# A chunk inverse with compacted blocks and wide transposes, and three smaller edits around it, in a fused hybrid decoder trunk

## Chip, cores and metric

One Trainium2 chip, one core. The metric is the device time of one launch in microseconds; lower is better. The kernel before takes 1242.85 us (median of 3 runs, 1240.87 to 1247.7).

## What is computed

Two residual layers on 512 tokens of width 1024, in float32. Only layer 0 matters here. Its input projection is split between an RWKV-7 time mix (8 heads of 64) and a stick-breaking attention (8 heads of 64); both outputs are concatenated and projected. A mixture of experts follows, then layer 1 (a gated linear recurrence) and a second mixture of experts.

```python
def rwkv7_time_mix(p, w0, decay_up, a0, iclr_up, gate_up, ...):
    ...
    w_log = -jax.nn.softplus(-(w0 + jnp.tanh(xw) @ decay_up)) - 0.5
    decay = jnp.exp(-jnp.exp(w_log))
    a = jax.nn.sigmoid(a0 + xa @ iclr_up)
    ...
    def step(S, inp):
        r_t, w_t, k_t, v_t, a_t, b_t = inp
        sa = jnp.einsum('bhvk,bhk->bhv', S, a_t)
        S = S * w_t[:, :, None, :] + sa[..., None] * b_t[:, :, None, :] + v_t[..., None] * k_t[:, :, None, :]
        return S, jnp.einsum('bhvk,bhk->bhv', S, r_t)
```

The kernel computes the recurrence in chunks of 64 tokens. Within a chunk the terms `sa` depend on one another through a strictly triangular 64x64 matrix, so each of the 64 chunk-and-head pairs (8 heads, 8 chunks) needs the inverse of a unit triangular 64x64 matrix.

## The kernel before, in words

Layouts. Two heads lie together on the 128 partitions (s = 0 on 0 to 63, s = 1 on 64 to 127). `AMa` holds the triangular matrices of all 4 head pairs and 8 chunks, 32 chunk slots of 2x64 columns. `ps` banks of PSUM are 128x512 float32, with tags: `pj` (2 banks, projections), `rw` (3 banks), `at` (2), `o` (1).

Order of layer 0. `norm_even` normalizes; `lora` (L368 to L395) makes the decay and rate gates; `pair` for 4 head pairs projects r, k, v and scales them, and its `chunks` (L478 to L498) makes the triangular matrices; `qkv` for 4 head pairs (L691 to L719) projects q, k and v of the attention; `inverse` (L500 to L553) inverts; `values` (L555 to L592) multiplies with v; then `step` and `attend` run together in an order that is written out by hand.

What sets the order. Outside that hand-written part a planner at build time interleaves what is independent, using estimates of each instruction's time; the source order is not the order of the queues. Each engine then works through its own queue strictly in that order. In the profile, `inverse` runs beside the projections of `qkv`, because the last head pair's matrices are ready early in `qkv`.

A projection is 24 matmuls (L325, L326, L327: 8 blocks of the contraction, each as high-high, high-low and low-high, since float32 is split into two parts). Its weights are cast by ScalarE (L297) and the remainder made by VectorE (L298). For q and k, `qkv` squares the result (L704), averages it over the head by a matmul (L706), takes Ln (L707) and Exp (L708) on ScalarE, and multiplies on VectorE (L709), which is what empties the `pj` bank. For v it copies (L715), transposes on TensorE (L718) and copies out of PSUM (L719, VectorE).

`inverse` has three parts:

- Diagonal blocks. The four 32x32 diagonal blocks of a pair's two matrices lie on the four 32-partition groups. Four 32-partition transposes (L511) bring them to `z`, one element of a block per partition. `XT` is set to the identity (L512, L513, GpSimd). Then 31 steps of a forward substitution, each a product with a broadcast row (L519) and a reduction (L521) over up to 31x31 elements, run on VectorE.
- Back. Six transposes (L528, four; L530, two) return the blocks to `AMa` and to `TT`.
- Off-diagonal blocks. 32x32 matmuls (L540), copies by ScalarE (L542), 32x32 matmuls (L549), copies by VectorE (L551).

`values` transposes v (L571, L575) into `UV`, then multiplies: one 128x128 product per pair and chunk (L585) computes both heads at once, of which the two diagonal 64x64 blocks are kept (L587 on ScalarE, L588 on VectorE); L591 clears the other halves of `AMa`.

`lora` keeps the two weight matrices (64 rows each) in one buffer padded by zeros to 128 rows, so that each product is a 128-row matmul (L388, L391), followed by a sigmoid (L389, L392).

Of the kernel before, what the change touches and what calls it, by code (L numbers as in the profile page):

```python
# [18 lines left out]
T = 512  # L19
# [140 lines left out]
class Kern:  # L160
# [207 lines left out]
    def lora(self):  # L368
        nc, ar, I = self.nc, self.ar, self.I
        self.L1, self.G1, self.G2 = ar.get(T), ar.get(T), ar.get(T)  # L370

        du = ar.get(2 * T)
        dv = du.f(2, T)
        nc.gpsimd.memset(dv[64:128, 0], 0.0)
        nc.gpsimd.memset(dv[0:64, 1], 0.0)
        nc.sync.dma_start(dv[0:64, 0], I["decay_up"][0])
        nc.sync.dma_start(dv[64:128, 1], I["iclr_up"][0])
        sig = []
        self.shifted(LORA, self.L1.f())
        sig.append(nc.scalar.activation(self.L1.f()[0:64], self.L1.f()[0:64], AF.Tanh))  # L380
        self.shifted(1664, self.G1.f())
        sig.append(nc.scalar.activation(self.G1.f(), self.G1.f(), AF.Sigmoid))
        self.shifted(1696, self.G2.f())
        sig.append(nc.scalar.activation(self.G2.f(), self.G2.f(), AF.Sigmoid))
        self.SG, self.AA = ar.get(4 * T), ar.get(4 * T)
        for p in range(4):
            z = self.bank("rw")
            nc.tensor.matmul(z, dv[:, 0, p * 128:p * 128 + 128], self.L1.f(), start=True, stop=True)  # L388
            sig.append(nc.scalar.activation(self.SG.f(4, T)[:, p], z, AF.Sigmoid, bias=self.v("w0", p)))  # L389
            z = self.bank("rw")  # L390
            nc.tensor.matmul(z, dv[:, 1, p * 128:p * 128 + 128], self.L1.f(), start=True, stop=True)  # L391
            sig.append(nc.scalar.activation(self.AA.f(4, T)[:, p], z, AF.Sigmoid, bias=self.v("a0", p)))  # L392
        du.free()
        self.L1.free()
        self.switch(sig)  # L395
# [104 lines left out]
    def inverse(self):  # L500
# [1 line left out]
        nc, ar = self.nc, self.ar  # L502
        X = [self.AMa.f(32, 2, 64)[:, :, s] for s in range(2)]

        Z, XT = ar.get(1024), ar.get(1024)
        z, xt = Z.f(32, 32), XT.f(32, 32)
        for G in range(4):
            q = slice(32 * G, 32 * G + 32)
            s, g = divmod(G, 2)
            src = X[s][q, :, 32 * g:32 * g + 32].rearrange("p c i -> p i c")  # L510
            nc.vector.transpose(z[q], src)  # L511
        nc.gpsimd.memset(XT.f(), 0.0)  # L512
        nc.gpsimd.memset(XT.f()[:, 0:1024:33], 1.0)  # L513
        tmp = ar.get(1024)
        for i in range(1, 32):

            w = i
            tv = tmp.f()[:, 0:i * w].rearrange("p (r j) -> p r j", r=w)
            nc.vector.tensor_tensor(tv, xt[:, 0:i, 0:w].rearrange("p j r -> p r j"),  # L519
                                    z[:, i:i + 1, 0:i].to_broadcast([128, w, i]), OP.mult)  # L520
            nc.vector.tensor_reduce(xt[:, i, 0:w], tv, AX.X, OP.add)  # L521
        tmp.free()
        Z.free()
        TT = ar.get(1024)
        for G in range(4):
            q = slice(32 * G, 32 * G + 32)
            s, g = divmod(G, 2)
            nc.vector.transpose(X[s][q, :, 32 * g:32 * g + 32].rearrange("p c i -> p i c"), xt[q])  # L528
            if g == 0:
                nc.vector.transpose(TT.f(32, 32)[q].rearrange("p c r -> p r c"), xt[q].rearrange("p i r -> p r i"))  # L530
        XT.free()

        W = ar.get(1024)
# [9 lines left out]
        for half in range(2):  # L543
            for s in range(2):
                b = self.bank("rw")
                lo, hi = slice(s * 64, s * 64 + 32), slice(s * 64 + 32, s * 64 + 64)
                for i in range(16):
                    c = half * 16 + i
                    nc.tensor.matmul(b[lo, i * 32:i * 32 + 32], W.f(32, 32)[hi, c], X[s][hi, c, 32:64],  # L549
                                     start=True, stop=True, tile_position=(s * 64 + 32, s * 64))  # L550
                nc.vector.tensor_copy(X[s][lo, half * 16:half * 16 + 16, 32:64], b[lo].rearrange("p (c i) -> p c i", c=16))  # L551
        W.free()
        TT.free()  # L553

    def values(self):  # L555
# [23 lines left out]
        RV, AM = self.RV.f(4, 8, 64), self.AMa.f(4, 8, 2, 64)  # L579
        for p in range(4):  # L580
            for g in range(2):
                b = self.bank("rw").rearrange("p (c s v) -> p c s v", c=4, s=2)
                for i in range(4):
                    c = g * 4 + i
                    nc.tensor.matmul(b[:, i].rearrange("p s v -> p (s v)"), AM[:, p, c].rearrange("p s i -> p (s i)"),  # L585
                                     UV[:, c, p].rearrange("p s v -> p (s v)"), start=True, stop=True)
                nc.scalar.activation(RV[0:64, p, g * 4:g * 4 + 4], b[0:64, :, 0], AF.Copy)  # L587
                nc.vector.tensor_copy(RV[64:128, p, g * 4:g * 4 + 4], b[64:128, :, 1])  # L588

            for s, e in enumerate((nc.gpsimd, nc.vector)):  # L590
                e.memset(AM[64 - s * 64:128 - s * 64, p, :, s], 0.0)  # L591
# [103 lines left out]
    def qkv(self, p):  # L695
# [20 lines left out]
        m = self.bank("at")  # L716
        for t in range(4):
            nc.tensor.transpose(m[:, t * 128:t * 128 + 128], v[:, t * 128:t * 128 + 128], self.ident)  # L718
        nc.vector.tensor_copy(self.VT[p].f(4, 128), m.rearrange("p (t x) -> p t x", t=4))  # L719

    def beside(self, p):

# [963 lines left out]
```

## Time and profile before

| | |
|---|---|
| median of 3 runs | 1242.85 us (1240.87 to 1247.7) |
| the profiled execution's own time | 1241.28 us |
| its span, first to last instruction | 1239.6 us |
| TensorE busy | 1166.2 us, 94% |
| VectorE busy | 1013.6 us, 82% |
| ScalarE busy | 795.6 us, 64% |
| GpSimd busy | 486.8 us, 39% |
| mean granted TensorE clock | 0.982 of full |

Durations are those of one profiled execution. A matmul's own duration includes its pipeline; the distance of two starts is what it costs in a row. PE is TensorE, PEld its weight loads, DVE VectorE, ACT ScalarE, POOL GpSimd, SP the engine that issues most DMAs. A float32 matmul shows as two passes.

### The profile page before, as it was taken

The page shows a single profiled execution, that of the slowest core. Times are in us where ns is not written, and L with a number is a line of the kernel's source. Part 1 is how long each engine was busy: PE and PEld are TensorE (multiplying, and loading weights), DVE is VectorE, ACT ScalarE, POOL GpSimd, SP SyncE. Part 2 cuts the span into 40 slices and gives each one's busy share as a digit, 9 for nine tenths or more (in the row PEclk, how much of TensorE's full clock was granted, in tenths as well). Part 3 has the DMA queues.
Part 4 walks back from the last instruction along what each step waited for, and adds up shares of the span by engine and source line. Part 5 has one row for each costly group of instructions (what it writes and reads, how often), then busy time and mean ns, then how long its engine had stood idle before and what let it go on. Part 6 is the DMA issues. An engine that isn't in the chain of part 4 may idle for free. (4 is left out here: it accounts for less than half of the span.)

```text
span 1239.6 us, 18201 instructions
## 1 busy us (share of the span) xinstructions
PE 1166.2 (94%) x6718; PEld 861.0 (69%) x6719; DVE 1013.6 (82%) x1292; ACT 795.6 (64%) x1063; POOL 486.8 (39%) x321
## 2 busy tenths in 40 slices
PE   6999998999998799999999899999988999999997
PEld 5777766877676577777776676677766777777764
DVE  5387899687767699999998565698667999999986
ACT  6533333388544688888888464566446888888883
POOL 8043200211011366677765211210113557767753
PEclk9999999899998899999999999999998999999999
DMA  6312221014965899999995612267478999999964
GB/s 170 85 51 68 68 68 35 2 26 138 342 238 209 282 343 364 355 357 354 355 347 186 187 51 68 69 203 269 162 250 311 342 365 366 345 346 352 345 232 147
DMA packets 152390, 274.45 MB, mean 221 GB/s; under 512 B 8172, under 2 KB 59053, under 8 KB 152295
## 3 DMA queue, kind: packets, MB, share of 16 engines
q1 hardware_dynamic: 142438, 247.85, 57.8%
q0 software_dynamic: 7840, 18.04, 6.2%
q10 hardware_dynamic: 2016, 7.34, 1.5%
q8 instruction: 54, 0.88, 0.3%
q14 instruction: 42, 0.34, 0.1%
HBM read 258.80 MB, written 22.28 MB: 227 GB/s over the span
## 5 line engine op out<-in xcount | busy, mean ns | idle before, releaser
L297 ACT ACTIVATE R<-A 128x1024 fp32r<-128x1024 f32 (+1 forms) x451 | 473.2, 1053 | 206.0 <-PE ps_pj L1362 67.2
L298 DVE TENSOR_TENSOR R<-A,R 128x1024 fp32r<-128x1024 f32 (+1 forms) x362 | 494.0, 1398 | 76.8 <-ACT R L297 72.9
L298 POOL TENSOR_TENSOR R<-A,R 128x1024 fp32r<-128x1024 f32 x89 | 257.3, 2890 | 245.5 <-ACT R L297 241.2
L1363 PE MATMUL ps_pj<-R 128*96 128x512 f32 x512 | 205.3, 401 | 9.9 <-DVE R L298 9.9
L1361 PE MATMUL ps_pj<-R 128*96 128x512 f32 x512 | 205.9, 402 | 0.0
L1362 PE MATMUL ps_pj<-R 128*96 128x512 f32 x512 | 204.0, 398 | 0.0
L325 PE MATMUL ps_pj<-R 128*128 128x512 f32 x296 | 121.7, 411 | 10.0 <-DVE A L709 9.3
L327 PE MATMUL ps_pj<-R 128*128 128x512 f32 x296 | 119.5, 404 | 3.5 <-DVE R L298 3.5
L326 PE MATMUL ps_pj<-R 128*128 128x512 f32 x296 | 121.1, 409 | 0.0
L1363 PEld LDWEIGHTS ps_pj<-R 128*96 128x96 f32 x512 | 84.1, 164 | 47.0 <-DVE R L298 10.8
L1362 PEld LDWEIGHTS ps_pj<-R 128*96 128x96 f32 x512 | 84.2, 164 | 35.4 <-DVE R L298 0.4
L1388 PE MATMUL ps_at<-R 128*96 128x512 f32 x256 | 103.7, 407 | 4.9 <-PEq L1583 1.8
L1361 PEld LDWEIGHTS ps_pj<-R 128*96 128x96 f32 x512 | 84.3, 165 | 33.9
L1389 PE MATMUL ps_at<-R 128*96 128x512 f32 x256 | 101.6, 397 | 0.0
L1390 PE MATMUL ps_at<-R 128*96 128x512 f32 x256 | 101.5, 397 | 0.0
L325 PEld LDWEIGHTS ps_pj<-R 128*128 128x128 f32 x296 | 56.5, 191 | 27.7 <-DVE A L709 11.3
L327 PEld LDWEIGHTS ps_pj<-R 128*128 128x128 f32 x296 | 56.4, 190 | 20.5 <-DVE R L298 5.7
L1397 POOL DMA_INDIRECT YD<-A x30 | 67.3, 2243 | 4.8 <-issue 2.2
L326 PEld LDWEIGHTS ps_pj<-R 128*128 128x128 f32 x296 | 56.5, 191 | 14.8 <-issue 4.1
L1164 POOL TENSOR_TENSOR A<-A 128x1024 f32<-128x1024 f32 x6 | 16.2, 2716 | 126.9 <-DVE A L870 87.3
L1266 DVE TENSOR_TENSOR A<-A 128x384 bf16<-128x384 f32 x32 | 60.0, 1886 | 0.0
L298 DVE TENSOR_TENSOR R<-ps_rw,R 128x384 fp32r<-128x384 f32 x92 | 47.7, 543 | 14.6 <-ACT R L297 14.5
(445 smaller groups left out, 2010.6 us busy)
## 6 DMA issues: line engine op xcount, KB each, us to landing
A<-in_exp_w_up_dram SPq DMA_DIRECT2D x61, 1024.0 KB
A<-in_exp_w_down_dram SPq DMA_DIRECT2D x61, 1024.0 KB
A<-in_exp_w_gate_dram SPq DMA_DIRECT2D x59, 1024.0 KB
A<-in_w_in_even_dram SPq DMA_DIRECT2D x27, 512.0 KB
A<-in_w_in_odd_dram SPq DMA_DIRECT2D x20, 512.0 KB
S<-in_exp_w_gate_dram SPq DMA_DIRECT2D x5, 1024.0 KB
A<-in_w_out_odd_dram SPq DMA_DIRECT2D x10, 512.0 KB
A<-in_x_dram SPq DMA_DIRECT2D x8, 512.0 KB
```

The source lines that it names most:

```text
L297: a = self.nc.scalar.activation(hi, src, AF.Copy)
L298: return a, (eng or self.nc.vector).tensor_tensor(lo, src, hi.bitcast(F32), OP.subtract)
L325: nc.tensor.matmul(p[0:n], hi[:, k], Hh[:, k], start=k == 0, stop=False)
L326: nc.tensor.matmul(p[0:n], hi[:, k], Hl[:, k], start=False, stop=False)
L327: nc.tensor.matmul(p[0:n], lo[:, k], Hh[:, k], start=False, stop=k == KD - 1)
L1361: self.nc.tensor.matmul(b, xh[:, k], hi, start=k == 0, stop=False)
L1362: self.nc.tensor.matmul(b, xl[:, k], hi, start=False, stop=False)
L1363: self.nc.tensor.matmul(b, xh[:, k], lo, start=False, stop=k == KD - 1)
L1388: nc.tensor.matmul(yb[n], hh[:, k], hi[:, cs], start=k == 0, stop=False)
L1389: nc.tensor.matmul(yb[n], hl[:, k], hi[:, cs], start=False, stop=False)
L1390: nc.tensor.matmul(yb[n], hh[:, k], lo[:, cs], start=False, stop=k == 3)
L1397: self.nc.gpsimd.indirect_dma_start(out=self.YD[l][:, :], out_offset=bass.IndirectOffsetOnAxis(ap=ix[0:SL], axis=0), in_=y.rearrange("p a ...
```

## The change

Four edits, all in layer 0:

- `lora`: the padded buffer is replaced by one of half the size, the two memsets go, and the two products of a step use 64 rows each, on the lower and the upper half of the array, into two banks taken together.
- `inverse`: ScalarE first copies the four diagonal blocks into one contiguous buffer (`tmp`), and one 128-partition transpose makes `z`. The result is kept by columns: the product now reads `xt` in sequence and the reduction writes a column with a step of 32 elements. One 128-partition transpose brings the result back into `tmp`, four ScalarE copies put the blocks into `AMa`, and one 128-partition transpose makes `TT`. Of the four copies out of PSUM at the end, two go to ScalarE.
- `values`: each 128x128 product becomes two of 128 rows by 64 columns, one per head, into the lower and upper half of the bank's partitions.
- `qkv`: the copy of v out of PSUM is done by ScalarE.

```diff
@@ lora
-        du = ar.get(2 * T)
-        dv = du.f(2, T)
-        nc.gpsimd.memset(dv[64:128, 0], 0.0)
-        nc.gpsimd.memset(dv[0:64, 1], 0.0)
-        nc.sync.dma_start(dv[0:64, 0], I["decay_up"][0])
-        nc.sync.dma_start(dv[64:128, 1], I["iclr_up"][0])
+        du = ar.get(T)
+        dv, q = du.f(), [slice(s * 64, s * 64 + 64) for s in range(2)]
+        for s, name in enumerate(("decay_up", "iclr_up")):
+            nc.sync.dma_start(dv[q[s]], I[name][0])
...
-            z = self.bank("rw")
-            nc.tensor.matmul(z, dv[:, 0, p * 128:p * 128 + 128], self.L1.f(), start=True, stop=True)
-            sig.append(nc.scalar.activation(self.SG.f(4, T)[:, p], z, AF.Sigmoid, bias=self.v("w0", p)))
-            z = self.bank("rw")
-            nc.tensor.matmul(z, dv[:, 1, p * 128:p * 128 + 128], self.L1.f(), start=True, stop=True)
-            sig.append(nc.scalar.activation(self.AA.f(4, T)[:, p], z, AF.Sigmoid, bias=self.v("a0", p)))
+            z = [self.bank("rw") for _ in q]
+            for s in range(2):
+                nc.tensor.matmul(z[s], dv[q[s], p * 128:p * 128 + 128], self.L1.f()[q[s]], start=True, stop=True)
+            for b, dst, name in zip(z, (self.SG, self.AA), ("w0", "a0")):
+                sig.append(nc.scalar.activation(dst.f(4, T)[:, p], b, AF.Sigmoid, bias=self.v(name, p)))
@@ inverse
-        for G in range(4):
-            q = slice(32 * G, 32 * G + 32)
-            s, g = divmod(G, 2)
-            src = X[s][q, :, 32 * g:32 * g + 32].rearrange("p c i -> p i c")
-            nc.vector.transpose(z[q], src)
+        diag = [(slice(32 * G, 32 * G + 32), G // 2, slice(32 * (G % 2), 32 * (G % 2) + 32)) for G in range(4)]
+        for q, s, g in diag:
+            nc.scalar.activation(tmp.f(32, 32)[q], X[s][q, :, g], AF.Copy)
+        nc.vector.transpose(z, tmp.f(32, 32).rearrange("p c i -> p i c"))
...
-            w = i
-            tv = tmp.f()[:, 0:i * w].rearrange("p (r j) -> p r j", r=w)
-            nc.vector.tensor_tensor(tv, xt[:, 0:i, 0:w].rearrange("p j r -> p r j"),
-                                    z[:, i:i + 1, 0:i].to_broadcast([128, w, i]), OP.mult)
-            nc.vector.tensor_reduce(xt[:, i, 0:w], tv, AX.X, OP.add)
-        tmp.free()
+            tv = tmp.f()[:, 0:i * i].rearrange("p (r j) -> p r j", r=i)
+            nc.vector.tensor_tensor(tv, xt[:, 0:i, 0:i], z[:, i:i + 1, 0:i].to_broadcast([128, i, i]), OP.mult)
+            nc.vector.tensor_reduce(xt[:, 0:i, i], tv, AX.X, OP.add)
+        nc.vector.transpose(tmp.f(32, 32).rearrange("p c i -> p i c"), xt.rearrange("p r i -> p i r"))
+        for q, s, g in diag:
+            nc.scalar.activation(X[s][q, :, g], tmp.f(32, 32)[q], AF.Copy)
         Z.free()
         TT = ar.get(1024)
-        for G in range(4):
-            q = slice(32 * G, 32 * G + 32)
-            s, g = divmod(G, 2)
-            nc.vector.transpose(X[s][q, :, 32 * g:32 * g + 32].rearrange("p c i -> p i c"), xt[q])
-            if g == 0:
-                nc.vector.transpose(TT.f(32, 32)[q].rearrange("p c r -> p r c"), xt[q].rearrange("p i r -> p r i"))
+        nc.vector.transpose(TT.f(32, 32).rearrange("p c r -> p r c"), xt)
+        tmp.free()
...
-                nc.vector.tensor_copy(X[s][lo, half * 16:half * 16 + 16, 32:64], b[lo].rearrange("p (c i) -> p c i", c=16))
+                (nc.vector.tensor_copy if s else nc.scalar.copy)(X[s][lo, half * 16:half * 16 + 16, 32:64], b[lo].rearrange("p (c i) -> p c i", c=16))
@@ values
-                b = self.bank("rw").rearrange("p (c s v) -> p c s v", c=4, s=2)
+                b = self.bank("rw")[:, 0:256].rearrange("p (c v) -> p c v", c=4)
                 for i in range(4):
                     c = g * 4 + i
-                    nc.tensor.matmul(b[:, i].rearrange("p s v -> p (s v)"), AM[:, p, c].rearrange("p s i -> p (s i)"),
-                                     UV[:, c, p].rearrange("p s v -> p (s v)"), start=True, stop=True)
-                nc.scalar.activation(RV[0:64, p, g * 4:g * 4 + 4], b[0:64, :, 0], AF.Copy)
-                nc.vector.tensor_copy(RV[64:128, p, g * 4:g * 4 + 4], b[64:128, :, 1])
+                    for s in range(2):
+                        nc.tensor.matmul(b[s * 64:s * 64 + 64, i], AM[:, p, c, s], UV[:, c, p, s], start=True, stop=True)
+                nc.scalar.activation(RV[0:64, p, g * 4:g * 4 + 4], b[0:64], AF.Copy)
+                nc.vector.tensor_copy(RV[64:128, p, g * 4:g * 4 + 4], b[64:128])
@@ qkv
-        nc.vector.tensor_copy(self.VT[p].f(4, 128), m.rearrange("p (t x) -> p t x", t=4))
+        nc.scalar.activation(self.VT[p].f(4, 128), m.rearrange("p (t x) -> p t x", t=4), AF.Copy)
```

## Rows read from the trace of the kernel before

**Rows 1.** The page, part 1: busy us of each engine.
```profile
PE 1166.2 (94%) x6718; PEld 861.0 (69%) x6719; DVE 1013.6 (82%) x1292; ACT 795.6 (64%) x1063; POOL 486.8 (39%) x321
```

**Rows 2.** Waits of TensorE, 0 to 300 us: total us, times, longest.
```profile
PE ps_pj L325 <- DVE A L709: 9.3, 3, 3.9
```

**Rows 3.** Windows: length, busy PE, PEld, DVE, ACT, POOL, clock, DMA share, GB/s.
```profile
149.20:226.30 77.10, 67.81 (x268) 50.99 (x266) 73.61 (x90) 22.88 (x33) 2.35 (x1) 0.93 0.16 43
226.30:235.70 9.40, 9.40 (x266) 8.98 (x265) 2.74 (x4) 3.79 (x6) 3.99 (x4) 0.97 0.01 3
```

**Rows 4.** Timeline, ScalarE and VectorE near the first stop: start, us.
```profile
164.15 0.63 ACT L708 ACTIVATE A<-A 128x512 f32<-128x512 f32 x1
...
169.48 0.74 DVE L709 SCALAR_TENSOR_TENSOR A<-ps_pj,A 128x512 f32<-128x512 f32 x1
```

**Rows 5.** Timeline, TensorE at the three stops: start, us, [idle before].
```profile
170.28 0.80 PE L325 MATMUL ps_pj<-R 128*128 128x512 f32 x1 [3.00 <-DVE A L709]
...
193.39 0.50 PE L325 MATMUL ps_pj<-R 128*128 128x512 f32 x1 [2.40 <-DVE A L709]
...
218.17 0.80 PE L325 MATMUL ps_pj<-R 128*128 128x512 f32 x1 [3.87 <-DVE A L709]
```

**Rows 6.** VectorE by line and shape: busy us, mean ns; 149 to 226, L551 later.
```profile
L511 DVE STREAM_TRANSPOSE A<-A 32x1024 f32<-32x1024 f32 x4 | 8.1, 2016 | 0.0
L528 DVE STREAM_TRANSPOSE A<-A 32x1024 f32<-32x1024 f32 x4 | 8.0, 1989 | 0.1
L530 DVE STREAM_TRANSPOSE A<-A 32x1024 f32<-32x1024 f32 x2 | 3.9, 1958 | 0.0
L519 DVE TENSOR_TENSOR A<-A 128x961 f32<-128x961 f32 x1 | 2.0, 1991 | 0.0
L719 DVE COPY S<-ps_at 128x512 f32<-128x512 f32 x2 | 1.4, 690 | 0.0
L521 DVE TENSOR_REDUCE A<-A 128x31 f32<-128x961 f32 x1 | 1.2, 1153 | 0.0
...
L551 DVE COPY A<-ps_rw 32x512 f32<-32x512 f32 x4 | 2.7, 684 | 2.2 <-PE ps_rw L549 2.2
```

**Rows 7.** Windows of L519 alone (first) and of L521 alone (second).
```profile
149.80:225.30 75.50, 23.81 (x31) 0.93 0.16 42
...
149.80:225.30 75.50, 15.61 (x31) 0.93 0.16 42
```

**Rows 8.** ScalarE by line and shape, 149 to 226 us.
```profile
L297 ACT ACTIVATE R<-A 128x1024 fp32r<-128x1024 f32 x9 | 9.6, 1062 | 29.7 <-PE ps_pj L326 29.7
```

**Rows 9.** Timeline: first and last of eight LoRA products, a sigmoid, two half-row products.
```profile
32.83 1.02 PE L388 MATMUL ps_rw<-A,S 128*128 128x512 f32 x2
...
38.83 1.02 PE L391 MATMUL ps_rw<-A,S 128*128 128x512 f32 x2
...
34.38 0.68 ACT L389 ACTIVATE A<-ps_rw,A 128x512 f32<-128x512 f32 x1
...
250.92 0.39 PE L754 MATMUL ps_at<-R 64*128 64x512 f32 x1
250.93 0.39 PE L754 MATMUL ps_pj<-R 64*128 64x512 f32 x1
```

**Rows 10.** Products of M and v, two state-step groups (timeline); their VectorE work (by shape).
```profile
242.24 7.38 PE L585 MATMUL ps_rw<-A 128*128 128x128 f32 x64
...
256.29 0.69 PE L621 MATMUL ps_rw<-A 128*64 128x64 f32 x16
256.81 0.64 PE L641 MATMUL ps_rw<-A 128*64 128x64 f32 x16
...
L588 DVE COPY A<-ps_rw 64x256 f32<-64x256 f32 x8 | 3.4, 428 | 1.6 <-ACT A L587 1.5
L591 DVE MEMSET A<- 64x512 f32 x4 | 1.9, 485 | 0.8 <-PE ps_rw L585 0.8
```

**Rows 11.** Waits of SP's queue, 225 to 420 us: the experts' weight loads.
```profile
SPq L1415 <- DVE R L298: 33.4, 8, 11.1
```

More of the change, by code (lines that the diff above doesn't have):

```diff
@@ L503, in inverse @@
         X = [self.AMa.f(32, 2, 64)[:, :, s] for s in range(2)]
-        Z, XT = ar.get(1024), ar.get(1024)
+        Z, XT, tmp = [ar.get(1024) for _ in range(3)]
         z, xt = Z.f(32, 32), XT.f(32, 32)
-        for G in range(4):
-            q = slice(32 * G, 32 * G + 32)
-            s, g = divmod(G, 2)
-            src = X[s][q, :, 32 * g:32 * g + 32].rearrange("p c i -> p i c")
-            nc.vector.transpose(z[q], src)
+        diag = [(slice(32 * G, 32 * G + 32), G // 2, slice(32 * (G % 2), 32 * (G % 2) + 32)) for G in range(4)]
+        for q, s, g in diag:
+            nc.scalar.activation(tmp.f(32, 32)[q], X[s][q, :, g], AF.Copy)
+        nc.vector.transpose(z, tmp.f(32, 32).rearrange("p c i -> p i c"))
         nc.gpsimd.memset(XT.f(), 0.0)
         nc.gpsimd.memset(XT.f()[:, 0:1024:33], 1.0)
-        tmp = ar.get(1024)
         for i in range(1, 32):
-            w = i
-            tv = tmp.f()[:, 0:i * w].rearrange("p (r j) -> p r j", r=w)
-            nc.vector.tensor_tensor(tv, xt[:, 0:i, 0:w].rearrange("p j r -> p r j"),
-                                    z[:, i:i + 1, 0:i].to_broadcast([128, w, i]), OP.mult)
-            nc.vector.tensor_reduce(xt[:, i, 0:w], tv, AX.X, OP.add)
-        tmp.free()
+            tv = tmp.f()[:, 0:i * i].rearrange("p (r j) -> p r j", r=i)
[4 more added lines that the diff above has]
+            nc.scalar.activation(X[s][q, :, g], tmp.f(32, 32)[q], AF.Copy)
         Z.free()
         TT = ar.get(1024)
-        for G in range(4):
-            q = slice(32 * G, 32 * G + 32)
-            s, g = divmod(G, 2)
-            nc.vector.transpose(X[s][q, :, 32 * g:32 * g + 32].rearrange("p c i -> p i c"), xt[q])
-            if g == 0:
-                nc.vector.transpose(TT.f(32, 32)[q].rearrange("p c r -> p r c"), xt[q].rearrange("p i r -> p r i"))
+        nc.vector.transpose(TT.f(32, 32).rearrange("p c r -> p r c"), xt)
+        tmp.free()
         XT.free()
```

## The prediction

> **What bounds the kernel now.** I read the page first: TensorE is busy for 94% of the span, VectorE for 82%, ScalarE for 64% [rows 1]. So time goes away only where TensorE waits, runs below full clock, or is given less to do. Next I read whom TensorE waits for in the first 300 us, the part that the diff touches. The largest item is one wait, three times, 9.3 us in all: the projections (L325) for the normalization of q and k on VectorE (L709), which empties the PSUM bank that the next projection needs [rows 2]. Third, the windows around the inverse [rows 3]. From 149.2 to 226.3 us the projections of q, k and v run beside the inverse. VectorE is busy 73.6 of 77.1 us, TensorE 67.8, at a mean granted clock of 0.93: a stage paced by VectorE. From 226.3 to 235.7 TensorE is full (the 32 by 32 products of the inverse).
>
> That VectorE is late, and not the chain of the normalization, is seen at the first stop: the Exp that L709 needs ends at 164.8 us, L709 starts only at 169.48 behind pieces of the inverse [rows 4], and TensorE, idle for 3.00 us by then, starts at 170.28 [rows 5]. The other stops are 2.40 and 3.87 us. After each the clock is down for a while: 0.07 of 77.1 us is 5.4 us of lost work, at most, as some of it may lie inside the stops. I take 5.0. [...]
>
> **The change, part by part.**
>
> Transposes. Ten narrow ones (32 partitions) go: 8.1 + 8.0 + 3.9 = 20.0 us of VectorE [rows 6]. Three wide ones (128 partitions) come. No row has a wide transpose. Lower bound: 1.2 us, what 1024 elements read in sequence would take by the 961-element reduction (1.15). Upper bound: four narrow ones, 8 us. I take 2.0 each, one narrow one, because elsewhere the partition count does not show (a 32x512 copy out of PSUM and a 128x512 one both take 0.69) [rows 6]. So 20.0 becomes 6.0: -14.0 (bounds -16.4 and +4). [...]
>
> Products of the recurrence. L519 takes 23.8 us in 31 pieces, the reductions (L521) over the same counts 15.6; at 961 elements 1.99 against 1.15 [rows 6, 7]. L519 reads one operand with a step of 32 elements, L521 reads in sequence. The change keeps the result by columns, so that L519 reads in sequence too and the reduction writes its few results with a step. I price L519 at L521's 15.6: -8.2 (bounds 0, if the broadcast operand is what is slow, and -8.2; the reduction's scattered writes are 1 in 31 elements, so I add nothing).
>
> Copies by ScalarE. Three of the four value copies (0.69 each) lie in this stage: -2.1 for VectorE [rows 6]. ScalarE takes these and eight 32x1024 copies, at 1.06 each by the 1024-element cast [rows 8]: 4.2 us ahead of the first transpose and 4.2 us behind the second. ScalarE is busy 22.9 of 77.1 us, so it has the room. The front four cost 4.2 + 2.0 = 6.2 where four transposes took 8.1, so the recurrence starts 1.9 earlier. The back four lie beside the third transpose; their cover is the rest of the projections. If that cover is gone, they are 4.2 us of waiting in front of L549.
>
> The stage. VectorE needs 73.6 - 14.0 - 8.2 - 2.1 = 49.3 us, TensorE 77.1 - 9.3 - 5.0 = 62.8 us. TensorE becomes the pace. But an in-order queue must also be early at the right place, so I walk the stops with today's order. At the first VectorE is 3.0 late and has gained 1.9 + 0.7 = 2.6. At the second it is 2.4 late, TensorE comes 4.7 earlier (first stop and its slow stretch), and VectorE has gained 1.9 + 1.4 and, an estimate, half of the 8.2: 7.4 against 7.1. At the third: 3.9 late plus 8.7, against 1.9 + 2.1 + 8.2 + 2 (three narrow transposes stood ahead of it, now two wide ones): 14.2 against 12.6. So the stops close, with little to spare at the first. I give 0.8 back: **-13.5**, bounds 0 and -14.7. What is late next is nothing on VectorE; the inverse should end some 5 us ahead of the last projection, and L540 and L549 stay 9.4 us of TensorE's own work.
>
> LoRA products. Today 8 fp32 products of 128 rows run alone on TensorE, two passes each, from 32.83 to 39.7: 6.9 us [rows 9]. With 64 rows, pairs on the two halves of the array into two banks run together, as L754 shows with starts 0.01 us apart [rows 9]: 3.4 us at best. But there are three banks, and each is emptied by a sigmoid of 0.68: 8 x 0.68 = 5.4, a gain of 1.5. Between 1.5 and 3.4 (if projections fill the holes) I take **-2.0**; nothing, if the pairs don't overlap. The stretch behind it, to 149 us, is TensorE's, so the gain stays. The two memsets on GpSimd and the allocation of half the size cost nothing: nobody waited for them.
>
> Products of M and v. 64 passes of 128x128 in 7.38 us become 128 passes of 128 rows by 64 columns. The same shape in the state steps starts 16 passes in 0.52 us (256.29 to 256.81) [rows 10], so 8 x 0.6 = 4.8: -2.6. But per pair of heads VectorE needs two copies of 0.43 and a memset of 0.49 [rows 10], 1.35, with gaps 1.45: 4 x 1.45 = 5.8: **-1.6**. I take this one; bounds 0 and -2.6. [...]
>
> Halving the last copies of the inverse (L551): the last of the four still follows the last product, so 0.
>
> Sum: -13.5 - 2.0 - 1.6 = -17.1. The profiled execution took 1241.28 us (span 1239.6), 1.6 below the median of the runs. 1242.85 - 17.1 = 1225.8, so **1226**. Later stages start earlier as a whole: the weight loads of the experts wait mostly for VectorE and the products around them to free their buffers [rows 11], so they move along.
>
> **Rivals.** (1) *Part of the queue's delay stays*: L519 is slow for its broadcast operand, or the planner's new order puts more of the inverse ahead of L709. Without the 8.2 VectorE gains 2.6 at the first stop and about 6 by the third, against 12.6: some 6 us of stops and slow clock survive, the stage gives -7, the whole -10.6: 1232. For it: no row reads L519's broadcast in sequence. Against: L521's step from 1.99 to 1.15 at equal counts. (2) *Nothing to see*: the order of instructions is laid out at build time by estimated durations; with more room it may bring the inverse forward and keep VectorE as late at L709 as now. The stage gives 0 to -3, with the other parts 1237 to 1242, within 0.5%. Against it: VectorE has then 13 us less to do than TensorE. (3) *Slower*: the planner moves L540 ahead of projections in TensorE's in-order queue because it counts on an early inverse. If VectorE then runs late, TensorE waits once, there, for the third transpose. It decides when the lag is larger than the projections left behind L540 cover. Price: the 14.3 of today's stops in one place, plus 2.0 + 2.0 + 4.2 for the transposes and the copies between, plus one more slow stretch (a third of the 5.0, 1.7), less 14.3, 2.0 and 1.6: +6, 1249. Against it: L709 holds TensorE and VectorE within a projection of each other.
>
> **How the numbers follow.** A measurement of this kernel tells about 0.5% (6.2 us) from no change. Forecast (1220 to 1230) 0.62, rival 1 (1230 to 1237) 0.18, rival 2 0.15, rival 3 0.05. Faster by over 0.5% is forecast and rival 1: 0.80; same 0.15; slower 0.05. The range goes from 1219 (all bounds: -14.7 - 3.4 - 2.6 = -20.7, and the runs' own spread) to 1239, which leaves out the upper half of rival 2 and rival 3. The likeliest case alone: 1220 to 1230.
>
> **What would show it.** Right: no wait of L325 for L709 over 1 us and a clock of 0.99 or more in the stage; three wide transposes of about 2 us; L519's largest near 1.15 us; the first L540 some 15 us earlier; the M and v products in under 6 us. Wrong: transposes at 8 us; L519 still 1.99; TensorE waiting at L540 or L549 for VectorE or ScalarE; L707 held up behind the 32x1024 copies.

## The result, and the profile after

The changed kernel takes 1228.51 us (median of 4 runs, 1227.72 to 1229.52), the kernel before beside it 1241.87 (4 runs, 1240.87 to 1247.7): 13.4 us or 1.1% less by medians; the ratio of the means is 0.9883, with a 95% interval of 0.9862 to 0.9904 (every ratio below is of that kind, against the kernel before). Forecast were 1226 and a range of 1219 to 1239. The profiled execution took 1228.33 us (span 1226.6), 0.2 under its median; that of the kernel before took 1241.28, 0.6 under the median of these runs.

The page of the changed kernel, part 1: TensorE is busy 6 us less than before, VectorE 27 us less, ScalarE 11 more [rows 1].

```profile
PE 1160.2 (95%) x6782; PEld 855.5 (70%) x6783; DVE 986.5 (80%) x1279; ACT 807.0 (66%) x1077; POOL 483.7 (39%) x319
```

The change shifts lines: in the code after, L709 is L700, L519 and L521 are L513 and L514, the three wide transposes L507, L515 and L520, the ScalarE copies L506 (front) and L517 (back), L540 is L531, L549 is L540, L585 is L577, and L388 and L391 are L387.

Waits of TensorE in the first 300 us of the changed kernel (total us, times, longest): what was 9.3 us in three stops [rows 2] is 0.6, and a stop of 1.5 us is new, at L697, the product that averages the square of q or k, for ScalarE (L695, which makes the square).

```profile
PE ps_at L697 <- ACT A L695: 1.5, 1, 1.5
...
PE ps_rw L562 <- DVE A L565: 0.8, 2, 0.5
...
PE ps_pj L325 <- DVE A L700: 0.6, 2, 0.3
PE ps_rw L577 <- DVE A L579: 0.6, 2, 0.4
PE ps_rw L612 <- DVE A L582: 0.6, 1, 0.6
```

Windows of the changed kernel, with the columns of [rows 3]: the projections until the first 32x32 product; then the stretch from there to the first attention product, cut near the places where the granted clock changes.

```profile
148.30:213.95 65.65, 63.39 (x268) 47.59 (x266) 50.70 (x81) 32.52 (x45) 2.38 (x1) 1.00 0.19 50
213.95:221.90 7.95, 7.95 (x224) 7.59 (x224) 0.45 (x1) 4.99 (x8) 2.92 (x3) 1.00 0.02 5
221.90:228.30 6.40, 6.06 (x63) 5.37 (x61) 3.71 (x6) 2.44 (x5) 1.80 (x1) 0.50 0.00 0
228.30:238.86 10.56, 8.56 (x166) 7.29 (x165) 7.15 (x18) 5.92 (x16) 2.08 (x4) 0.98 0.01 2
```

The stage of the projections went from 77.1 to 65.7 us; VectorE, which paced it with 73.6 busy us, now has 50.7, and TensorE is busy for 63.4 at full clock. Behind it, TensorE drops to half its clock (granted 0.50) from 221.9 to 228.6 us, in the 32x32 products and the v transposes; before, the low clock lasted from 235.2 to 238.5 in that stretch.

VectorE's work of that stage in the changed kernel, by line and shape (busy us, mean ns):

```profile
L515 DVE STREAM_TRANSPOSE A<-A 128x1024 f32<-128x1024 f32 x1 | 2.2, 2234 | 0.0
L507 DVE STREAM_TRANSPOSE A<-A 128x1024 f32<-128x1024 f32 x1 | 2.1, 2099 | 2.5 <-ACT A L506 2.5
L520 DVE STREAM_TRANSPOSE A<-A 128x1024 f32<-128x1024 f32 x1 | 1.9, 1928 | 0.0
...
L514 DVE TENSOR_REDUCE A<-A 128x31 f32<-128x961 f32 x1 | 1.2, 1157 | 0.0
L513 DVE TENSOR_TENSOR A<-A 128x961 f32<-128x961 f32 x1 | 1.2, 1153 | 0.0
```

A transpose of 128 partitions costs what one of 32 did (1.93 to 2.23 against 1.96 to 2.02), and the product takes what the reduction takes.

One account serves all runs below: the span is cut at the first attention product, and the time ahead of it into the three places that the change touches.

| us | before | after | change |
|---|---|---|---|
| LoRA: first product to the next projection's second | 7.09 | 6.41 | -0.7 |
| projections of q, k, v (to the first 32x32 product) | 77.07 | 65.65 | -11.4 |
| from there to the first attention product | 24.32 | 24.91 | +0.6 |
| first attention product at | 250.58 | 238.86 | -11.7 |
| rest of the span | 989.0 | 987.7 | -1.3 |

(The three rows lack 0.2 us of shifts between them.) In all but one of the runs below the rest lies between 986.9 and 989.1 (991.6 in that one), whatever was edited: what is saved ahead of the attention passes through to the end, and the 1.3 us in the rest is within that spread.

### The profile page after: what moved, and what is told of

It reads as the page before. It is cut to its first block, busy times and chain, and to the rows that moved or that the text cites. A ratio compares the mean times of both kernels' runs of the same rounds, so it can differ in the third digit from the quotient of the medians.

```text
span 1226.6 us, 18324 instructions
## 1 busy us (share of the span) xinstructions
PE 1160.2 (95%) x6782; PEld 855.5 (70%) x6783; DVE 986.5 (80%) x1279; ACT 807.0 (66%) x1077; POOL 483.7 (39%) x319
## 3 DMA queue, kind: packets, MB, share of 16 engines
q1 hardware_dynamic: 142438, 247.85, 58.5%
## 5 line engine op out<-in xcount | busy, mean ns | idle before, releaser
L327 PE MATMUL ps_pj<-R 128*128 128x512 f32 x296 | 118.3, 400 | 3.5 <-DVE R L298 3.5
L325 PE MATMUL ps_pj<-R 128*128 128x512 f32 x296 | 119.4, 403 | 1.5 <-DVE A L700 0.6
L326 PE MATMUL ps_pj<-R 128*128 128x512 f32 x296 | 119.4, 403 | 0.0
L327 PEld LDWEIGHTS ps_pj<-R 128*128 128x128 f32 x296 | 55.6, 188 | 20.0 <-DVE R L298 5.7
L325 PEld LDWEIGHTS ps_pj<-R 128*128 128x128 f32 x296 | 55.6, 188 | 19.2 <-issue 3.4
L326 PEld LDWEIGHTS ps_pj<-R 128*128 128x128 f32 x296 | 55.6, 188 | 14.3 <-issue 3.6
```

The lines of the kernel that those rows point to most:

```text
L325: nc.tensor.matmul(p[0:n], hi[:, k], Hh[:, k], start=k == 0, stop=False)
L326: nc.tensor.matmul(p[0:n], hi[:, k], Hl[:, k], start=False, stop=False)
L327: nc.tensor.matmul(p[0:n], lo[:, k], Hh[:, k], start=False, stop=k == KD - 1)
```

## The experiments

Each is an edit of the changed kernel. "Stage" is the projections, "tail" the stretch from the first 32x32 product to the attention. Medians of timed runs; the changed kernel's is 1228.51.

### Rows in place of columns

```diff
-            nc.vector.tensor_tensor(tv, xt[:, 0:i, 0:i], ...)
-            nc.vector.tensor_reduce(xt[:, 0:i, i], tv, AX.X, OP.add)
+            nc.vector.tensor_tensor(tv, xt[:, 0:i, 0:i].rearrange("p j r -> p r j"), ...)
+            nc.vector.tensor_reduce(xt[:, i, 0:i], tv, AX.X, OP.add)
```

The second and third transpose read `xt` the other way round accordingly; all else stays, and on TensorE, VectorE and ScalarE the instructions stand in the same order as in the changed kernel.

> The changed kernel with the result of the recurrence kept by rows again, so that its products read with a step of 32 elements; transposes stay wide, and the order of instructions on TensorE, VectorE and ScalarE is the same as in the changed kernel. Theory (an in-order queue has to be early at the right place): the products take 23.8 us again instead of 15.6, VectorE 58.9 us of a stage of 65.6, and although that is less than TensorE needs, L700 comes late again behind them: stops of 5 to 7 us in all plus slow clock, time 6 to 9 us above the changed kernel, about 1236. Rival (only totals count, TensorE needs 63.3 us and VectorE less): at most 1 us above, 1229.

Measured: 1238.94 us (12 runs, 1234.89 to 1241.31), ratio 0.9971 (0.9957 to 0.9985): 10.4 us slower than the changed kernel, a little over the theory's 6 to 9. Its form with 961 elements on VectorE, its waits of TensorE and its stage:

```profile
L513 DVE TENSOR_TENSOR A<-A 128x961 f32<-128x961 f32 x1 | 2.0, 1952 | 0.0
```

```profile
PE ps_pj L325 <- DVE A L700: 5.7, 4, 3.2
PE ps_at L697 <- ACT A L695: 2.8, 1, 2.8
```

```profile
148.58:222.09 73.51, 64.97 (x268) 48.61 (x266) 58.51 (x81) 32.52 (x45) 2.38 (x1) 0.98 0.17 46
225.00:239.00 14.00, 13.66 (x188) 12.34 (x185) 4.13 (x6) 4.46 (x9) 2.86 (x4) 0.53 0.01 1
```

The same product with its operand strided is back at 1.95 us. VectorE has 58.5 busy us in a stage where TensorE needs 65.0, and still TensorE stops for 8.5 us: busy totals do not decide, the place in the queue does. That the order did not change also suggests that the planner's estimates give the strided read no price of its own, so nothing was moved to make up for it. The stage is 7.9 us longer; 2.9 more lie in the tail, where the low clock lasts from 225.8 to 239.5. So the layout by columns alone carries 7.9 of the 11.4 us that the stage gained, about the 8.2 us of VectorE work that it saves. The 2.9 of the tail come by a clock whose fall no run here explains, and are not shown to be the layout's. The rival, that only totals count, is wrong.

### Ten narrow transposes and no ScalarE copies, columns kept

```diff
-            nc.scalar.activation(tmp.f(32, 32)[q], X[s][q, :, g], AF.Copy)
-        nc.vector.transpose(z, tmp.f(32, 32).rearrange("p c i -> p i c"))
+            nc.vector.transpose(z[q], X[s][q, :, g].rearrange("p c i -> p i c"))
```

The way back likewise: four transposes into `X`, two into `TT`.

> The changed kernel with the ten narrow transposes of before and no ScalarE copies of the blocks; columns stay. Theory: VectorE carries 14 us more, 64.6 us against 63.3 of TensorE, with 8.1 of it ahead of the recurrence and 12 behind it: stops of L325 for the multiplication of q and k return, time 5 to 9 us above the changed kernel, about 1235. Rival (the products by columns were what mattered, the transposes are hidden): within 2 us of the changed kernel, 1229 to 1230.

Measured: 1232.66 us (6 runs, 1231.85 to 1233.86), ratio 0.9925 (0.9909 to 0.9942): 4.2 slower, a little less than the theory's least and twice the rival's most. The stage:

```profile
148.27:216.71 68.44, 64.02 (x268) 48.90 (x266) 64.70 (x88) 24.67 (x36) 2.37 (x1) 0.98 0.19 49
```

VectorE is the pace again, by a hair (64.7 against 64.0 us), with stops of 4.4 us, and the stage is 2.8 longer; the tail 1.4. Of 14 us that VectorE has less to do with wide transposes only 2.8 count in the stage, because the columns alone had already brought VectorE level with TensorE.

### The whole old inverse in the changed kernel

```diff
-        for q, s, g in diag:
-            nc.scalar.activation(tmp.f(32, 32)[q], X[s][q, :, g], AF.Copy)
-        nc.vector.transpose(z, tmp.f(32, 32).rearrange("p c i -> p i c"))
+            nc.vector.transpose(z[q], src)
...
```

`inverse` is the one before the change, with its rows, ten transposes and L551; the other three edits stay.

> The changed kernel with the whole inverse as it was before (narrow transposes, products by rows, no ScalarE copies of blocks); the LoRA products, the products of M and v and the value copies stay changed. Theory (the inverse carries nearly all): the three stops come back, the projections take about 75 us instead of 65.65, and the kernel is only 1.5 to 2.5 us below the kernel before, 1240. Rival (the smaller edits carry a third or more): 1237 or less.

Measured: 1242.88 us (10 runs, 1237.39 to 1244.7), ratio 0.999 (0.9969 to 1.001): no gain is left, and 2.9 more than the theory's 1240. Its waits of TensorE and its windows (stage and tail; L706 there is L700):

```profile
PE ps_pj L325 <- DVE A L706: 10.3, 3, 4.3
```

```profile
148.20:227.11 78.91, 68.60 (x268) 51.52 (x266) 72.20 (x88) 24.67 (x36) 2.70 (x1) 0.91 0.16 42
227.11:254.32 27.21, 25.41 (x447) 22.69 (x446) 12.82 (x26) 12.43 (x26) 6.80 (x8) 0.75 0.01 2
```

The LoRA stretch is 6.42 us, so its 0.7 is there, but TensorE waits longer for VectorE (10.3 against 9.3 us). The M and v products take 7.19 us to the attention (247.13 to 254.32) as against 8.34 before, so their gain is there too. Both are taken back: the stage is 1.8 us longer than before, and from the first 32x32 product to the first M and v product this run needs 20.0 us, the kernel before 16.0, with the low clock lasting from 230.6 to 244.2 us; the whole tail runs at a mean clock of 0.75 in place of 0.93. Of the 14.4 us between this run and the changed kernel 13.3 lie in the stage. So the inverse carries the stage's gain; that the small edits are worth nothing is not what the total of this run shows.

### Who does the four copies behind the second transpose

The new stop at L697 is ScalarE's queue. Timeline of the changed kernel, ScalarE and then TensorE (start, us, [idle before]):

```profile
200.28 1.06 ACT L517 ACTIVATE A<-A 32x1024 f32<-32x1024 f32 x1 [4.80 <-DVE A L515]
201.24 0.57 ACT L695 ACTIVATE A<-ps_pj 128x512 f32<-128x512 f32 x1
...
201.87 1.12 PE L697 MATMUL ps_at<-A 128*128 128x512 f32 x2 [1.53 <-ACT A L695]
```

ScalarE stands idle for 4.8 us at the first back copy (L517), which waits for the transpose on VectorE. L695, which TensorE needs, is next in its queue; the projection that it squares had ended at 200.1, so it could have started some 1.1 us earlier. Two runs move the copies to another engine:

```diff
-            nc.scalar.activation(X[s][q, :, g], tmp.f(32, 32)[q], AF.Copy)
+            nc.vector.tensor_copy(X[s][q, :, g], tmp.f(32, 32)[q])
```

> The changed kernel with the four copies of the inverted blocks back into AMa done by VectorE instead of ScalarE. Theory (the 1.5 us for which TensorE waits at the averaging of q's square are ScalarE standing behind such a copy, while VectorE idles there): that wait goes, time 1 to 2 us lower, about 1227. Rival (VectorE then comes late for the remainder of the weights or for L700): no gain or up to 2 us more, 1229 to 1231.

Measured: 1228.93 us (5 runs, 1228.0 to 1229.83), ratio 0.9895 (0.9877 to 0.9914): no gain. The stop at L697 is gone and one of the same length stands at L700, behind the copies that VectorE now does; the stage is 65.03. The wait of this kernel, and the window of its 32x32 products, of which more below:

```profile
PE ps_pj L325 <- DVE A L700: 2.0, 2, 1.6
```

```profile
213.24:222.62 9.38, 9.38 (x266) 8.96 (x265) 0.69 (x1) 5.58 (x9) 3.93 (x4) 0.98 0.01 3
```

```diff
-            nc.scalar.activation(X[s][q, :, g], tmp.f(32, 32)[q], AF.Copy)
+            nc.gpsimd.tensor_copy(X[s][q, :, g], tmp.f(32, 32)[q])
```

> The changed kernel with the four copies of the inverted blocks back into AMa done by GpSimd, which has nothing to do there. Theory (ScalarE standing behind those copies is what TensorE waits for at L697, and VectorE's own copies only moved that wait to L700): both waits go, the stretch of the projections takes 63.5 to 64 us instead of 65.65, time about 1227. Rival (the copies are slow on GpSimd and are still not done when the 32x32 products need them, or VectorE and GpSimd slow each other): a wait at L531 or L540, 1229 or more.

Measured: 1228.21 us (4 runs, 1226.19 to 1231.36), ratio 0.9879 (0.9854 to 0.9903). Stage and tail:

```profile
148.71:211.98 63.27, 62.74 (x268) 47.66 (x266) 50.95 (x81) 28.41 (x41) 7.40 (x5) 1.00 0.20 53
211.98:238.29 26.31, 24.14 (x447) 21.33 (x447) 11.31 (x24) 13.35 (x28) 6.79 (x8) 0.81 0.01 2
```

GpSimd, with 2.4 us of work in this stage, takes the copies, the waits at L697 and L700 shrink to 0.4 in all, and the stage is 2.4 us shorter, all that the theory asked. TensorE hardly pauses there now (busy for 62.7 of 63.3). But the tail is 1.4 longer at a mean clock of 0.81 against 0.86, and the total shows nothing. The stop is shown to cost 1.5 to 2.4 us in its stage; that the total would fall by it is not shown by this run.

### The copy of v back on VectorE

```diff
-        nc.scalar.activation(self.VT[p].f(4, 128), m.rearrange("p (t x) -> p t x", t=4), AF.Copy)
+        nc.vector.tensor_copy(self.VT[p].f(4, 128), m.rearrange("p (t x) -> p t x", t=4))
```

> The changed kernel with the copy of v out of PSUM back on VectorE. Theory (with the inverse shortened VectorE has 13 us to spare, and only its place in the queue counts): L700 comes 0.7 us later per head pair, the stops grow from 0.6 to at most 2 us, time 0 to 2 us above the changed kernel. Rival (VectorE still paces the stage): 2.1 us or more above.

Measured: 1229.16 us (4 runs, 1227.5 to 1230.3), ratio 0.9895 (0.9863 to 0.9927): 0.65 more, within the runs. One stop is traded for the other (1.6 us for L700, and 0.3 in place of 1.5 at L697). With VectorE no longer the pace, its 2.1 us are free.

### The LoRA pair in two pools of banks

```diff
-            z = [self.bank("rw") for _ in q]
+            z = [self.bank(tag) for tag in ("rw", "at")]
```

> The changed kernel with the second product of each LoRA pair put into the banks of the attention, idle at that time, so that five banks rotate instead of three. Theory (the LoRA pairs gain only 0.7 us because the next product waits for a sigmoid to empty its bank, and the sigmoids start late behind a weight cast and a shift on ScalarE): from the first LoRA product to the next projection 4 to 4.5 us instead of 6.4, time about 2 us lower, 1226.5. Rival (products on the two halves of the rows don't overlap, or ScalarE holds up the projection behind them as well): 6 us or more there, no gain.

Measured: 1229.74 us (4 runs, 1227.34 to 1233.89), ratio 0.9898 (0.9871 to 0.9925). The stretch went from 6.41 to 5.83 us only, not to the 4 to 4.5 of the theory, and the total cannot tell 0.6 us. Timeline of ScalarE in the changed kernel, with the banks as they were:

```profile
32.51 1.06 ACT L297 ACTIVATE R<-A 128x1024 fp32r<-128x1024 f32 x1 [1.79 <-PE ps_pj L326]
33.48 0.67 ACT L338 ACTIVATE A<-ps_pj,A 128x511 f32<-128x511 f32 x1
34.04 1.83 ACT L389 ACTIVATE A<-ps_rw,A 128x512 f32<-128x512 f32 x3
35.75 0.64 ACT L382 ACTIVATE S<-S 128x512 f32<-128x512 f32 x1
36.27 3.18 ACT L389 ACTIVATE A<-ps_rw,A 128x512 f32<-128x512 f32 x5
```

TensorE's first product starts at 32.58, the first sigmoid only at 34.04, behind a weight cast and a shift, and another activation (L382) stands between the sigmoids. Five banks in place of three are worth 0.6 us; what is left is ScalarE's. The rival's first half is ruled out: in the run with five banks the two products of a pair start 0.01 us apart.

```profile
33.01 0.59 PE L387 MATMUL ps_rw<-A,S 64*128 64x512 f32 x1
33.02 0.59 PE L387 MATMUL ps_at<-A,S 64*128 64x512 f32 x1
```

### The copies of the M and v products shared out

```diff
-                nc.vector.tensor_copy(RV[64:128, p, g * 4:g * 4 + 4], b[64:128])
+                (nc.scalar.copy if g else nc.vector.tensor_copy)(RV[64:128, p, g * 4:g * 4 + 4], b[64:128])
```

> The changed kernel with every second copy of the products of M and v on the upper half of the partitions done by ScalarE instead of VectorE. Theory (this stage is paced by emptying PSUM on VectorE, 1.35 us per head pair against some 1.2 of TensorE): the waits for L579 and L582, 1.4 us in all, mostly go, time about 1 us lower, 1227.5. Rival (the last clearing memset or the next step's first wait decides): no change, 1228.5.

Measured: 1227.65 us (4 runs, 1226.07 to 1229.37), ratio 0.988 (0.9858 to 0.9903). From the first v transpose to the attention 13.86 us against 14.83, the 1.0 that was expected there; the total moves by as little as the runs differ among themselves, so the total does not settle it. The products of M and v in the two kernels, on TensorE's timeline, the changed kernel first:

```profile
231.68 2.30 PE L577 MATMUL ps_rw<-A 128*64 128x64 f32 x64
234.40 1.62 PE L577 MATMUL ps_rw<-A 128*64 128x64 f32 x48 [0.42 <-DVE A L579]
236.19 0.69 PE L577 MATMUL ps_rw<-A 128*64 128x64 f32 x16 [0.17 <-DVE A L579]
...
238.60 0.33 PE L612 MATMUL ps_rw<-A 128*64 128x64 f32 x2 [0.58 <-DVE A L582]
238.86 0.50 PE L745 MATMUL ps_at<-R 64*128 64x512 f32 x1
```

```profile
233.04 4.73 PE L577 MATMUL ps_rw<-A 128*64 128x64 f32 x128
```

With both engines emptying PSUM the 128 passes run without a stop, in 4.7 us; the prediction gave 4.8 as TensorE's own need.

### The inverse ahead of the last q, k, v group

```diff
+            if p == 3:
+                self.inverse()
...
-        self.inverse()
```

> The changed kernel with the inverse called ahead of the last head pair's projections instead of behind them, so that the planner lays its 32x32 products between those projections. Theory (the 32x32 products and the transposes of v run at a clock of 0.65 to 0.98 because they stand alone; between projections the clock stays near 1.0): from the start of the projections to the first product of the attention 86 to 88 us instead of 90.6, time 1225. Rival (TensorE now waits at the first 32x32 product for the third transpose, with the projections behind it in the queue): a wait of 2 us or more at L531, and no gain or a loss, 1228 to 1232.

Measured: 1231.09 us (4 runs, 1229.95 to 1233.23), ratio 0.9895 (0.9873 to 0.9917): 2.6 slower. TensorE at the first 32x32 product, and the two low stretches behind it:

```profile
202.23 3.98 PE L531 MATMUL ps_rw<-A 32*32 32x32 f32 x90 [2.20 <-DVE A L520]
```

```profile
203.40:210.00 6.60, 6.60 (x73) 5.80 (x69) 0.00 (x0) 3.03 (x5) 0.00 (x0) 0.50 0.01 2
213.50:223.40 9.90, 9.90 (x101) 7.92 (x98) 5.12 (x5) 4.03 (x6) 1.80 (x1) 0.50 0.01 2
```

This is the mechanism of the prediction's rival 3, made to happen: TensorE waits in one place for the third transpose. It costs 2.2 us, not the 24.2 that the rival put in one place (14.3 + 8.2 + 1.7): the lag of 14.3 is no longer there. The theory of this run is wrong: from the start of the projections to the attention it takes 93.9 us, not 86 to 88, and the clock is now low in the middle of the projections too. The rival had both the wait and the time.

### Two combinations

```diff
+            z = [self.bank(tag) for tag in ("rw", "at")]
...
+                (nc.scalar.copy if g else nc.vector.tensor_copy)(RV[64:128, p, g * 4:g * 4 + 4], b[64:128])
...
+            if p == 3:
+                self.inverse()
```

> The early inverse, the LoRA products over five banks and the shared copies of the products of M and v together. Theory: their gains add, 2 + 3 + 1 us below the changed kernel, about 1223. Rival (each gain is taken back by a wait at the attention's start or by the clock): within 2 us of the changed kernel.

Measured: 1234.61 us (6 runs, 1228.66 to 1235.59), ratio 0.9917 (0.9895 to 0.9938), against an expectation near 1223. The wait of 2.2 us at the first 32x32 product is there again; the attention starts at 241.20 us and the rest takes 991.6. The expectation took the early inverse for a gain, and the run above shows that it is a loss; the other two edits do not make up for it. The rival, within 2 us of the changed kernel, is off as well.

```diff
-            z = [self.bank("rw") for _ in q]
+            z = [self.bank(tag) for tag in ("rw", "at")]
...
-            nc.scalar.activation(X[s][q, :, g], tmp.f(32, 32)[q], AF.Copy)
+            nc.gpsimd.tensor_copy(X[s][q, :, g], tmp.f(32, 32)[q])
...
-                nc.vector.tensor_copy(RV[64:128, p, g * 4:g * 4 + 4], b[64:128])
+                (nc.scalar.copy if g else nc.vector.tensor_copy)(RV[64:128, p, g * 4:g * 4 + 4], b[64:128])
```

> The changed kernel with block copies back on GpSimd, LoRA products over five banks and the shared copies of the products of M and v. Theory (small gains add, the clock in the 32x32 stretch takes part of it back): 1226, 2 us below the changed kernel. Rival (the low clock takes all of it): 1228 to 1229.

Measured: 1225.59 us (4 runs, 1223.25 to 1227.1), ratio 0.9871 (0.9839 to 0.9903), the fastest of all: 2.9 below the changed kernel by medians, and no run of the one reaches the other's. The two ratios' intervals overlap, so the lead is likely rather than settled. Stage and tail:

```profile
148.07:211.33 63.26, 62.79 (x267) 47.65 (x265) 50.92 (x81) 28.42 (x41) 7.41 (x5) 1.00 0.20 53
211.33:234.53 23.20, 21.01 (x446) 18.79 (x445) 9.94 (x20) 14.82 (x32) 6.79 (x8) 0.93 0.01 2
```

The stage's 2.4 us (63.26 against 65.65) are kept here, where the clock of the tail is 0.93 and not 0.81 as with the GpSimd copies alone. The tail's own 1.7 us (23.20 against 24.91) are the shared copies, worth 1.0 above, and the clock.

### Wide products among the 32x32 ones

The low clock begins within the 32x32 products. The question is whether wide products among them keep it up. After every eighth 32x32 product a 128x512 product is added whose result nobody reads; this run does more work than the kernel.

```diff
+        fill = lambda: nc.tensor.matmul(o, hh[:, 0, 0:128], hh[:, 1], start=True, stop=True)
...
+                    if i % 8 == 7:
+                        fill()
```

> The changed kernel with one extra full-width 128x512 product behind every eighth 32x32 product, 16 in all, into an unused PSUM bank; their results are never read. Theory (it is the stretch of 32x32 products itself after which the clock falls, not a wait): no fall behind it, granted clock 1.00, and from the first 32x32 product to the attention's first product 25.3 us (24.9, plus 16 x 0.23 for the extra products, less some 3.2 of low clock). Rival (a wait or the transposes of v cause the fall): the clock falls as before, 28 us or more there, time 3 to 4 us above the changed kernel.

Measured: 1242.81 us (10 runs, 1242.0 to 1247.83), ratio 1.0016 (0.9996 to 1.0037). TensorE's timeline at full clock (L526 is the added product, L533 the 32x32 ones), and the windows of the stretch before and after the fall:

```profile
214.91 0.49 PE L526 MATMUL ps_o<-R 128*128 128x512 f32 x1
215.34 0.69 PE L533 MATMUL ps_rw<-A 32*32 32x32 f32 x16
215.95 0.50 PE L526 MATMUL ps_o<-R 128*128 128x512 f32 x1
```

```profile
214.30:222.20 7.90, 7.90 (x129) 5.93 (x129) 0.00 (x0) 3.83 (x6) 2.36 (x1) 1.00 0.01 3
222.20:239.70 17.50, 17.50 (x166) 13.10 (x165) 3.44 (x5) 2.49 (x5) 1.80 (x1) 0.51 0.00 1
```

The clock falls at 222.5 all the same and stays at half (0.50 of full) for 17 us. The theory is wrong: the stretch to the attention takes 38.2 us, not 25.3. The rival has the fall, but not the time: the run is 14.3 us above the changed kernel, not 3 to 4. The price of the filling was missed too: one group (16 passes and a wide product) takes 1.04 us, start to start, of which the 16 passes are 0.50 (96 passes run in 3.02 us in the changed kernel), so 0.54 for a product that costs 0.23 among its like (the 128x512 products of the projection just ahead start 0.23 us apart).

## Why the prediction was right, and where its terms were off

**The mechanism** is as forecast. VectorE no longer paces the projections: TensorE's waits of L325 for L700 are 0.6 us in all, the clock of the stage is 1.00, and TensorE needs 63.4 us (estimated: 62.8). The gain of the column layout is shown by the run with rows (7.9 of the stage's 11.4 us), that of the wide transposes with their copies by the run with narrow ones (2.8), that of all of the inverse by the run with the old one. One sign fell short: the first 32x32 product comes 12.3 us earlier, not some 15.

**Transposes: right.** Priced at 2.0 us each, they take 2.23, 2.10 and 1.93. The upper end, four narrow ones, was far off. What these rows show is that this transpose (1024 float32 elements per partition) takes on 128 partitions what it took on 32 (1.96 to 2.02).

**Products of the recurrence: right.** L513 takes 1.153 at 961 elements beside the reduction's 1.157, and 15.8 us in all (priced at 15.6). The reduction's scattered writes cost nothing here: L514 takes 15.6 us in all by columns, L521 took 15.6 by rows [rows 7]. VectorE's stage was put at 49.3 us and is 50.7. (Of the three value copies in that sum [rows 6] shows two; the trace has the third at 160.41 us, so the sum stands.) The broadcast operand, on which rival 1 rested, is the same in the run with rows, where only the step of the other operand, 32 elements, makes 1.95 us of the 1.153, a factor of 1.7; rival 1 falls. No run tries another step, so what in the read costs this is not shown.

**Stage: -13.5 forecast, -11.4 measured.** The failed step is "it has the room": ScalarE's busy share was counted (22.9 us before, 32.5 of 65.7 now), its queue was not walked. The front copies cost what was said (1.06 us each); the back ones were taken as covered by the projections and priced only "in front of L549". What they hold up is L695 behind them in the in-order queue, and through it L697: a stop of 1.5 us. With the copies on GpSimd the stage measures 63.27, within 0.3 us of the forecast (77.1 - 13.5 = 63.6): TensorE is idle for 0.5 us in place of 2.3 and busy for 0.65 less, the latter unexplained. The prediction walked VectorE's queue; for ScalarE's it named one sign, L707 held up behind the copies, and did not walk it. It was the square (L704 then, L695 now) that was held up.

**LoRA: -2.0 forecast, -0.7 measured.** The eight sigmoids take 5.4 us from the first start to the last end (34.04 to 39.45), the number that was priced, but by luck: the price had them one behind the other at 0.68, while the first three start 0.57 us apart and another activation (L382) stands among them. And the term counted them from the first product, while ScalarE reaches them 1.5 us later. The failed step is the start of the sum, not its size.

**M and v products: -1.6 forecast, -1.2 measured.** From the first product to the attention 8.34 us became 7.18. The products themselves take 5.0 us in place of 7.4, with stops of 0.6 us for VectorE's copies (L579): the products became shorter, the copies out of PSUM did not (0.42 us each on VectorE, 0.43 before). What was not in the sum is a further 0.8 us of the next products (L612) waiting for VectorE's copy and its memset (L582).

**The tail: 0 forecast, +1.75 measured** ahead of the M and v products. The prediction kept it as "TensorE's own work" and left its clock out. The 32x32 products take 10.08 us against 9.43, without an idle moment in either kernel, at a clock of 0.89 against 0.97:

```profile
213.95:224.03 10.08, 10.08 (x266) 9.65 (x265) 0.69 (x1) 5.57 (x9) 4.46 (x4) 0.89 0.01 4
```

The v transposes take 7.65 against 6.55, at a clock of 0.70 against 0.78; 0.5 of these 1.1 us are waits of L562 for VectorE's copies (0.8 in two stops, 0.3 in one before), so the clock's share of the 1.75 is some 1.2.

**Halved last copies and the copy of v: 0** were forecast. For the copy of v its own run shows it; no run tests the halved copies by themselves.

**The sum.** -11.7 at the attention's start and -1.3 behind it make -13.0 of span, -13.4 by medians, for -17.1 forecast: 2.1 lost in the stage, 1.3 in LoRA, 0.4 at M and v, and 1.75 in the tail make up 5.6; the 0.2 at the seams and the 1.3 behind go the other way. The later stages do move along, as forecast. Rival 2 (nothing to see) is ruled out by the interval and by the stage's 11.4 us; its own sum was off, as 0 to -3 with the other parts' -3.6 gives 1236 to 1239, not 1237 to 1242. Rival 3 showed its mechanism only when forced, at 2.2 us.

## What to carry to other kernels

Sharing work out to an engine with a low busy share needs the same walk as the late engine itself: look what stands behind each moved instruction in the new engine's queue, and which engine waits for that (a copy that waited 4.8 us for its input held up what stood behind it, and TensorE stopped for 1.5 us, on an engine that was half idle). When a stage is paced by VectorE, look first at the step of its innermost reads: the same product took 1.95 us with a step of 32 elements and 1.15 in sequence, and a layout turned round was worth 7.9 us of its stage, about as much as the work saved, although VectorE's total had fitted into TensorE's without it. A gain in one stage can be taken back in the next, where the clock is lower (with the copies on GpSimd the stage took 2.4 us less, the tail 1.4 more at a mean clock of 0.81 against 0.86), so cut the span at fixed instructions and compare stretch by stretch before you believe or dismiss a small difference in the total.

## What was not expected of the hardware

**The clock falls in a stretch without a stop.** In every run but one TensorE goes to half its clock (granted 0.50) within the 32x32 products, though between the first of them and the fall it does not pause (in the changed kernel it is busy for all of these 7.9 us, at 1.00). Only with the inverse early does a stop, of 2.2 us, stand just ahead of them; in the combination with the early inverse, the one exception, the clock falls some 0.2 us before the first of them. The fall came 7.9 us after the first 32x32 product in the changed kernel, 9.0 in the run with copies on VectorE (9.38 us for the same products, clock 0.98, against 10.08 and 0.89), 3.7 with rows, 2.8 with copies on GpSimd, 1.0 with the inverse early; the low stretch lasted from 3 us to 17. The run with rows has the same order of instructions as the changed kernel, so the order does not set the moment. Wide products in between did not prevent it. What sets the moment and the length stays open: no run here tells it. It blurs the small edits: in the runs that leave the tail's instructions alone the tail takes from 0.7 us less (copies on VectorE) to 2.9 more (rows) than in the changed kernel.

**A wide product among 32x32 ones costs more.** A 128x512 product between groups of 32x32 ones cost 0.54 us, among its like 0.23: some 0.3 us more. The tile size changes twice there, from 32x32 to 128x128 and back; no run here separates that from what else changes at these places, such as the weight load.
